# Who begins the copies of the kept weight sums, and a third seven-product unit in the attention's output projection

## The chip, the cores and the metric

The kernel runs on one core of one Trainium2 chip. The metric is device time in microseconds (us), the median of several executions. Engines are named as the profile names them: PE (TensorE, matmuls; PEld is its weight load), DVE (VectorE), ACT (ScalarE), POOL (GpSimd) and SP (SyncE, which here only begins DMA transfers). ACT and POOL can begin transfers too. Sixteen DMA engines carry the transfers of all three.

## The reference

Two layers of a pre-norm encoder trunk over 256 tokens of width 2048, all float32, and a last RMSNorm. Cut to what matters:

```python
h = x
for i in range(2):
    a = rms_norm(h, mix_norm[i])
    mixed = neighborhood_attention(a, na_w_qkv, na_rpb, na_w_o) if i == 0 \
            else short_conv_mixer(a, sc_w_in, sc_conv_w, sc_w_out)
    h = h + mixed
    h = h + conv_glu_ffn(rms_norm(h, ffn_norm[i]), ffn_w_up[i], ffn_conv_w[i],
                         ffn_conv_b[i], ffn_w_down[i])
return rms_norm(h, final_norm)
# attention: 16 heads of 128; output projection out (256x2048) @ w_o (2048x2048)
# ffn: up 2048 -> 2 x 5632, conv over 3 positions, silu(g)*u, down 5632 -> 2048
```

## The kernel before, in words

**Split products.** Every weight is read from HBM once per use and split on the chip into a high part `hi` (a rounding to float32r by ACT, line 186) and a low part `lo` (the rest, by DVE, line 189). Activations are split too. A product of two 128x128 by 128x512 blocks is then three matmuls: hi by hi, hi by lo, lo by hi (lines 463 to 465).

**Chunks.** Weights come in chunks, each loaded by SP into a tile `raw` (six buffers, 128x1024 at most) and then split into `hi` and `lo` tiles. The list `chunks` is in order of use. `prep_to(n)` writes out the loads and splits up to chunk n; the main loop calls it ahead of every item of PE's work, so that 4 chunks (AHEAD) or, in the up-projections and the short-convolution input, 6 chunks (FURTHER) are prepared ahead of the one in use. A load must wait until the splits have read the buffer that it fills. Each engine executes its own instructions in the order written; a planner sets this order, and `issue_after` ties an instruction behind a named one on the same engine.

**Phases.** Projections in which the weights stand still run as `Phase` (lines 262 and 270): q and k of the attention, the short convolution's input, and each FFN's up-projection in two halves. In a `Phase` an item is two output tiles of 128 channels, four chunks. v runs as `Values`, a pair of k blocks per item.

**Output projections** (attention's w_o, short convolution's w_out, and four half down-projections) run as `Tokens`: the activations stand still, 512 weight columns move. One group g covers 1024 output columns, in a left and a right half, and a unit is a pair of k blocks. An ordinary unit, P in the plans, takes eight block products in two chunks (left, right). A seven-product unit, H in the plans, is one step of Winograd's form of Strassen's method over two k blocks, two token blocks and two column halves: seven products instead of eight. It needs sums of weight blocks (the kept sums), sums of the activation blocks (`forms`, four adds on POOL, then a split), and four more PSUM accumulators `mu`, which `combine` adds into the result h once the last H unit of a group is done. `due` in the plan says how many ticks later that is written out. An H unit has three chunks: the left half, the second block of the right half, and the kept sums, whose loads fill two raw buffers (512 KB and 256 KB) and whose last sum is ended by one add on DVE (line 151).

**Kept sums.** The weight sums are made in DRAM by DMA, one job for each H unit and group (67 jobs). `make` writes a job out: three copies of 256 KB from the weight to the kept tile, later two transfers that add another block to them (`first`, 8 chunks later, ADDS) and one that adds a kept row to another (`second`, 16 chunks later). All six are begun by POOL, in POOL's own order (`pool`, line 217). The planning takes the jobs from one list, `jobs`, in order of use, and spreads them over earlier stages: QK_JOBS, V_JOBS, UP_JOBS and SC_JOBS say how many in each, and `hosts` over which items. Between these transfers POOL has the bias sums of the attention and the `forms`, each of which waits for a result of DVE or ACT; ahead of such a wait POOL issues whatever stands in its queue.

**Attention's tail.** `mix` (line 646 on) ends a pair of heads: PSUM tile o, split by ACT and DVE into `oT`, and for the pairs named in S_ATT a copy on ACT (line 667) and `make_forms`. The pairs of heads are the units of the output projection: unit 5 is heads 10 and 11. PSUM tiles `st`, `sc`, `tr`, `o` are used by the attention first and then by the `mu` sums. After a group of `Tokens` its results are added to h (line 360, `residual`), and this must be done before PE may start the next group on the same four PSUM tiles.

Of the kernel before, what the change touches and what calls it, by code (L numbers as in the profile page):

```python
# [26 lines left out]
NH = 16  # L27
# [18 lines left out]
def plan(text, due):  # L46


    words = text.split()
    return (tuple(int(x[1:]) for x in words), {int(x[1:]) for x in words if x[0] == "H"}, due)  # L50
# [4 lines left out]
S_MLP = {(0, 0): S_FIRST, (0, 1): (S_SECOND, S_SECOND),  # L55
         (1, 0): S_FIRST, (1, 1): (plan("P0 P2 H1 H3 H4 P9 H5 H6 H7 H8 P10", 0), plan("P0 P2 H1 H3 H4 P5 H6 H7 H8 P9 P10", 0))}
S_OUT = (plan("P0 H1 H2 P3 H4 H5 P6 P7", 1), plan("P0 P3 H1 H2 P6 H4 H5 P7", 0))
S_ATT = (plan("P0 P1 P2 H6 P3 H7 P4 P5", 1),) * 2
QK_JOBS, V_JOBS, UP_JOBS, SC_JOBS = (0, 2, 2, 0), (2, 2, 2, 0), (11, 11, 10, 11), 14


HEAD = (2, 4)
# [18 lines left out]
def trunk(ctx, tc, xT, par, bias, wqk, wv, wo, wsc, wscout, wup, wdown, out):  # L81
    nc = tc.nc
# [109 lines left out]
    kept, newest, fenced = {}, {}, []  # L192

    def make(w, g, i):

        kept[id(w), g, i] = dst = dp.tile([P, 3, 4 * P], F32, name=f"kept{len(kept)}")
        l, r, t = (w[8 * g + f:8 * g + f + 4, :, (2 * i + k) * P:(2 * i + k + 1) * P].rearrange("f p c -> p f c")
                   for f, k in ((0, 0), (4, 0), (4, 1)))
        at = [dst[:, n].rearrange("p (f c) -> p f c", f=4) for n in range(3)]
        for n, x in ((0, l), (1, t), (2, t)):  # L200
            pool(nc.gpsimd.dma_start, out=at[n], in_=x)

        def first():
            for n in range(2):
                pool(nc.gpsimd.dma_start, out=at[n], in_=r, accum_op=ALU.add)

        def second():
            pool(nc.gpsimd.dma_start, out=at[2], in_=at[0], accum_op=ALU.add)
        stores.append((len(prepped) + ADDS, first))
        stores.append((len(prepped) + 2 * ADDS, second))  # L210

    def pool(op, **of):

        with ExitStack() as order:
            if "POOL" in newest:
                order.enter_context(tc.issue_after(newest["POOL"].ins))
            newest["POOL"] = op(**of)  # L217
# [3 lines left out]
    def plan_jobs(w, plans):  # L221
        jobs.extend((w, g, i) for g, (order, sset, _) in enumerate(plans) for i in order if i in sset)

    def take(n):
        out, jobs[:] = jobs[:n], jobs[n:]
        return out
# [58 lines left out]
    at = [0]  # L285
# [19 lines left out]
    def split(dst, src):  # L305
        return split_into(dst[:, :S], dst[:, S:], src)
# [6 lines left out]
    def act_tile():  # L313
        return ap_.tile([P, 2 * S], F32R, name="act", tag="act", bufs=HALF)

    def a_tile():
        return ap_.tile([P, 2 * S], F32R, name="a", tag="a", bufs=KT)
# [202 lines left out]
    def make_forms(xe, xo, place, fresh=False):  # L520

        if fresh:
            form_at[:], left_over[:] = ("sf", "vv", "qk") * 2, ()
        v = tp.tile([P, 4, P], F32, name="s", tag="s")
        x11, x21, x12, x22 = (x[:, t * P:(t + 1) * P] for x in (xe, xo) for t in range(2))
        pool(nc.gpsimd.tensor_sub, out=v[:, 0, :], in0=x21, in1=x22)
        pool(nc.gpsimd.tensor_sub, out=v[:, 1, :], in0=v[:, 0, :], in1=x11)
        pool(nc.gpsimd.tensor_add, out=v[:, 3, :], in0=x12, in1=v[:, 1, :])
        pool(nc.gpsimd.tensor_sub, out=v[:, 2, :], in0=x11, in1=x21)
        if isinstance(place, tuple):  # L530
            hi, lo = place
            split_into(hi, lo, v.rearrange("p f c -> p (f c)"))
            return [(hi[:, j * P:(j + 1) * P], lo[:, j * P:(j + 1) * P]) for j in (0, 1, 3, 2)]

        blocks = 3 if place else 4
        y = form_slots(blocks)
        if isinstance(y, list):
            at = [(x[:, :P], x[:, P:]) for x in y]
            to = [(*at[j], v[:, j]) for j in range(3)]
        else:  # L540
            y = y.rearrange("p (b t c) -> p t b c", t=2, c=P)
            at = [(y[:, 0, j], y[:, 1, j]) for j in range(blocks)]
            to = [(y[:, 0, :blocks], y[:, 1, :blocks], v[:, :blocks])]
        if place:
            at.append((place[:, P:2 * P], place[:, 3 * P:]))
            to.append((*at[3], v[:, 3]))

        def splits():
            for x in to:
                split_into(*x)  # L550
        after(LATE, splits)
        return [at[j] for j in (0, 1, 3, 2)]
# [4 lines left out]
    def to_norm(n, a):  # L557

        ssq = ep.tile([P, 2, KT // 4], F32, name=f"ssq{n}")

        def evac(t, q, ps):
            added = residual(t, q, ps)
            squares(t, q, ssq)

            def next_input():
                for k0, tag in zip(range(4 * q - 4, 4 * q + 4, 2), ("tr", "o", "sc", "st")):
                    tr = transposed(k0, tag)
                    for k in range(2):
                        a[k0 + k] = a_tile()
                        scaled_split(a[k0 + k], tr[:, k, :], norm_g(n, k0 + k))  # L570
            if t and q % 2:
                after(1, next_input)
                if q == KT // 4 - 1:
                    after(2, lambda: spread_factor(token_factor(ssq)[0]))
            return added
        return evac
# [6 lines left out]
    oT = [None] * NH  # L583
# [67 lines left out]
    def mix(hs, v):  # L651

        o = pa.tile([P, 2, S], F32, name="o", tag="o")
        for i, h in enumerate(hs):
            for k in range(2):
                p = heads[h]["pT"][k]
                vh, vl = (x[:, h % 4 * P:(h % 4 + 1) * P] for x in v[k])
                nc.tensor.matmul(o[:, i, :], lhsT=vh, rhs=p[:, :S], start=k == 0, stop=False)
                nc.tensor.matmul(o[:, i, :], lhsT=vh, rhs=p[:, S:], start=False, stop=False)
                nc.tensor.matmul(o[:, i, :], lhsT=vl, rhs=p[:, :S], start=False, stop=k == 1)  # L660
        for i, h in enumerate(hs):
            oT[h] = act_tile()
            split(oT[h], o[:, i, :])
            heads[h].clear()
        if hs[0] // 2 in S_ATT[0][1]:
            x = tp.tile([P, 2, S], F32, name="s", tag="s")
            nc.scalar.copy(out=x, in_=o)

            place = (a_tile(), a_tile()) if hs[0] // 4 == NH // 4 - 1 else oT[hs[0]]
            oforms[hs[0] // 2] = make_forms(x[:, 0, :], x[:, 1, :], place)  # L670

    class Values:
# [175 lines left out]
    def mlp(layer, a, evac):  # L848
        for half in range(2):
            act, forms = [None] * HALF, {}  # L850
            lo = half * HALF
            Phase(wup[layer], [f for j in range(lo, lo + HALF) for f in (2 * j, 2 * j + 1)], KT, a,
                  up_evac(layer, act, forms, S_MLP[layer, half]), intro=0 if half else 3,
                  jobs=take(UP_JOBS[2 * layer + half]), hosts=(1, 20) if half else (4, 25))
            Tokens(down[layer, half], HALF, act, evac if half else residual, S_MLP[layer, half], forms,
                   halves=4 if half and layer else 0)

    down = {(layer, half): wdown[layer, half] for layer in range(2) for half in range(2)}
    plan_jobs(wo, S_ATT)
    for half in range(2):  # L860
# [4 lines left out]
    for g in range(NH // 4):  # L865
        Phase(wqk, range(8 * g, 8 * g + 8), KT, a0, qk_evac, intro=0 if g else INTRO, step=STEP,
              jobs=take(QK_JOBS[g]), hosts=(0, 4))
        Values(g, a0, take(V_JOBS[g]))
    Tokens(wo, KT, oT, to_norm(1, a1), S_ATT, oforms)
    mlp(0, a1, to_norm(2, a2))  # L870
# [52 lines left out]
    for item[0], (ph, ft, c, k0, ka, kb) in enumerate(items):  # L923

        with ExitStack() as order:
# [4 lines left out]
            if item[0] != KT // STEP * INTRO:  # L930
# [3 lines left out]
                end, n = ends[item[0]], FURTHER if getattr(ph, "fence", False) else AHEAD  # L934
# [77 lines left out]
```

## Time and profile before

| | us |
|---|---|
| median of 3 runs | 2210.82 (2210.37 to 2211.88) |
| the profiled execution, its time | 2210.34 |
| its span, first to last instruction | 2208.4 |
| PE busy | 2184.2 (99%) |
| DVE busy | 1744.9 (79%) |
| ACT busy | 1307.3 (59%) |
| POOL busy | 468.3 (21%) |

How to read it: the profile is one execution. Its page gives busy time by engine, forty slices of the span, the DMA queues, the chain of work that ended last, and the costliest groups of instructions. A busy PE is not PE at full rate: a 128x512 matmul is shown with some 391 ns, but matmuls overlap in the pipeline, so the rate is read from the starts of successive ones. The queue q1 holds what SP begins, q10 what ACT begins, q0 what POOL begins. A wait is put down to the releaser that came last.

The stages in the order of time: q, k and v up to 304 us, the attention's output projection up to 401, the first FFN (up, down, up, down) up to 1128, the short convolution up to 1481, the second FFN up to the end.

### The profile page before, as it was taken

The numbers are of one execution on the slowest core, as the hardware profiler recorded it, in microseconds if no ns is written. First come the engines' busy times: TensorE is split into PE (matmuls) and PEld (weight loads), VectorE is DVE, ScalarE is ACT, GpSimd is POOL, SyncE is SP. The second block draws the span as 40 slices with busy tenths as digits, with TensorE's granted clock in tenths as the row PEclk, the third lists the DMA queues.
The fourth block names the chain that finished last, engine by engine and source line by source line (L and its number), as shares of the span: only waits on it lengthen the run. The fifth ranks groups of instructions, "written<-read, shape, count | busy, mean of one in ns | idle before, by whom it ended". The sixth has DMA issues, their size and how long they took to land.

```text
span 2208.4 us, 33010 instructions
## 1 busy us (share of the span) xinstructions
PE 2184.2 (99%) x11707; PEld 1890.4 (86%) x11707; DVE 1744.9 (79%) x2664; ACT 1307.3 (59%) x1996; POOL 468.3 (21%) x561
## 2 busy tenths in 40 slices
PE   9999999999999999999999999999999999999998
PEld 8888887888888888887788888888888888888886
DVE  8777676877788887876986666888778898777898
ACT  7555555655566655654775544566556666555665
POOL 1343120024330023234001323101241100242200
PEclk9999999999999999999999999999999999999999
DMA  8999758688998879999876999966989887899885
GB/s 274 272 284 254 217 181 242 202 252 239 272 271 281 283 213 274 276 255 304 280 250 180 291 259 293 303 220 193 283 237 276 268 269 248 264 247 270 238 275 182
DMA packets 330389, 561.61 MB, mean 254 GB/s; under 512 B 22064, under 2 KB 219824, under 8 KB 330224
## 3 DMA queue, kind: packets, MB, share of 16 engines
q1 hardware_dynamic: 232368, 453.46, 60.3%
q0 software_dynamic: 96480, 105.41, 24.7%
q8 instruction: 92, 1.51, 0.3%
q10 hardware_dynamic: 1376, 0.63, 0.1%
q14 instruction: 73, 0.60, 0.1%
HBM read 557.32 MB, written 107.48 MB: 301 GB/s over the span
## 4 chain that ended last, share of the span: by engine, by line
PE 94%; DMA 2%; DVE 2%; ACT 1%; issue 1%; DVEq 0%; ACTq 0%
PE mm L262 42%; PE mm L270 22%; PE mm L463 6%; PE mm L464 6%; PE mm L465 6%; PE mu L463 2%; PE mu L465 2%; PE mu L464 2%; PE mm L693 1%; PE mm L694 1%; PE mm L695 1%; DVE lo L189 1%; DMA raw<-in_wo 1%; DMA raw<-in_wdown 1%; PE tr L371 1%
## 5 line engine op out<-in xcount | busy, mean ns | idle before, releaser
L189 DVE TENSOR_TENSOR lo<-raw,hi 128x1024 fp32r<-128x1024 f32 (+1 forms) x859 | 1021.0, 1214 | 194.0 <-PE mm L270 93.5
L186 ACT CAST hi<-raw 128x1024 fp32r<-128x1024 f32 (+1 forms) x926 | 923.4, 1010 | 421.1 <-PE mm L465 103.0
L262 PE MATMUL mm<-a,hi 128*128 128x512 f32 x4096 | 961.8, 391 | 0.5 <-DVE a L310 0.3
L262 PEld LDWEIGHTS mm<-a,hi 128*128 128x128 f32 x4096 | 759.7, 188 | 152.9 <-DVE a L310 1.2
L270 PEld LDWEIGHTS mm<-a,lo 128*128 128x128 f32 x4096 | 512.9, 192 | 11.8
L270 PE MATMUL mm<-a,lo 128*128 128x256 f32 x4096 | 518.1, 283 | 0.0
L217 POOL DMA_DIRECT2D kept<-in_wdown x275 | 276.5, 1672 | 88.8 <-DMA kept<-in_wdown 82.2
L463 PE MATMUL mm<-hi,act 128*128 128x512 f32 x620 | 243.4, 393 | 8.1 <-DVE h L360 7.4
L465 PE MATMUL mm<-hi,act 128*128 128x512 f32 x620 | 242.1, 391 | 0.0
L217 POOL TENSOR_TENSOR s<-conv 128x128 f32<-128x128 f32 x56 | 26.3, 470 | 952.1 <-DVE conv L752 952.1
L339 ACT ACTIVATE conv<-pad,pt 128x256 f32<-128x256 f32 x176 | 105.7, 601 | 194.7 <-DVE pad L331 194.5
L464 PE MATMUL mm<-lo,act 128*128 128x512 f32 x558 | 218.4, 391 | 0.9 <-DVE lo L189 0.8
L341 DVE SCALAR_TENSOR_TENSOR conv<-pad,pt,conv 128x256 f32<-128x256 f32 x384 | 185.2, 484 | 40.0 <-ACT conv L339 24.5
L325 ACT COPY corr<-mm 128x256 f32<-128x256 f32 x256 | 93.1, 369 | 135.8 <-PE mm L270 135.1
L463 PEld LDWEIGHTS mm<-hi,act 128*128 128x128 f32 x620 | 117.0, 189 | 34.1 <-issue 6.9
L465 PEld LDWEIGHTS mm<-hi,act 128*128 128x128 f32 x620 | 117.0, 189 | 24.3
L464 PEld LDWEIGHTS mm<-lo,act 128*128 128x128 f32 x558 | 105.4, 189 | 23.1 <-DVE lo L189 1.6
L302 DVE TENSOR_TENSOR act<-conv,act 128x256 fp32r<-128x256 f32 x88 | 37.7, 428 | 96.0 <-ACT act L301 96.0
L326 DVE TENSOR_TENSOR corr<-mm,corr 128x256 f32<-128x256 f32 x256 | 107.2, 420 | 5.6 <-ACT corr L325 5.5
L217 POOL DMA_DIRECT2D kept<-kept x67 | 70.6, 1072 | 126.6 <-DMA kept<-in_wdown 98.6
L463 PE MATMUL mu<-hi,sf 128*128 128x512 f32 x189 | 74.5, 394 | 1.9 <-ACT hi L186 1.9
L464 PE MATMUL mu<-lo,sf 128*128 128x512 f32 x189 | 74.6, 395 | 1.2 <-DVE lo L189 1.2
(156 smaller groups left out, 1658.0 us busy)
## 6 DMA issues: line engine op xcount, KB each, us to landing
raw<-in_wup SPq DMA_DIRECT2D x352, 512.0 KB, 6.3
kept<-in_wdown POOLq DMA_DIRECT2D x275, 256.0 KB, 12.9
raw<-in_wdown SPq DMA_DIRECT2D x121, 512.0 KB, 5.1
raw<-in_wsc SPq DMA_DIRECT2D x96, 512.0 KB, 6.4
raw<-kept SPq DMA_DIRECT2D x67, 512.0 KB, 5.5
raw<-in_wqk SPq DMA_DIRECT2D x56, 512.0 KB, 6.9
kept<-kept POOLq DMA_DIRECT2D x67, 256.0 KB, 8.5
raw<-kept SPq DMA_DIRECT2D x67, 256.0 KB, 4.9
```

The lines of the kernel that those rows point to most:

```text
L186: newest["ACT"] = nc.scalar.copy(out=hv, in_=r)
L189: newest["DVE"] = nc.vector.tensor_sub(out=lv, in0=r, in1=hv.bitcast(F32))
L217: newest["POOL"] = op(**of)
L262: nc.tensor.matmul(self.ps[ft], lhsT=prepped[i][0][:, o:o + P], rhs=self.src[k], start=k == 0, stop=False)
L270: nc.tensor.matmul(self.ps[ft][:, S:], lhsT=prepped[i][1][:, o:o + P], rhs=self.src[k][:, :S], start=False, stop=k == self.nk - 1)
L325: nc.scalar.copy(out=corr, in_=ps[:, S:])
L326: nc.vector.tensor_add(out=corr, in0=ps[:, :S], in1=corr)
L339: nc.scalar.activation(c, x[:, 1:S + 1], AF.Identity, scale=w[1], bias=b)
L341: nc.vector.scalar_tensor_tensor(out=c, in0=x[:, tap:tap + S], scalar=w[tap], in1=c, op0=ALU.mult, op1=ALU.add)
L463: nc.tensor.matmul(ps, lhsT=xh, rhs=wh, start=start, stop=False)
L464: nc.tensor.matmul(ps, lhsT=xh, rhs=wl, start=False, stop=False)
L465: nc.tensor.matmul(ps, lhsT=xl, rhs=wh, start=False, stop=stop)
```

## The change

Three things are edited. The three copies of each job are begun by ACT, tied behind the newest hi split that was written out, instead of by POOL in POOL's order; the adding transfers stay on POOL. The attention's output projection gets a third H unit, unit 5, in both groups, another order of units, and `due` 0 instead of 1; that makes 69 jobs instead of 67, and the two more are taken in the second half of the first FFN's up-projection. The forms of unit 5 get two `act` tiles of their own.

```diff
-S_ATT = (plan("P0 P1 P2 H6 P3 H7 P4 P5", 1),) * 2
-QK_JOBS, V_JOBS, UP_JOBS, SC_JOBS = (0, 2, 2, 0), (2, 2, 2, 0), (11, 11, 10, 11), 14
+S_ATT = (plan("P0 P1 H5 P2 H6 P3 H7 P4", 0),) * 2
+QK_JOBS, V_JOBS, UP_JOBS, SC_JOBS = (0, 2, 2, 0), (2, 2, 2, 0), (11, 13, 10, 11), 14
...
         for n, x in ((0, l), (1, t), (2, t)):
-            pool(nc.gpsimd.dma_start, out=at[n], in_=x)
+            with tc.issue_after(newest["ACT"].ins):
+                nc.scalar.dma_start(out=at[n], in_=x)
...
-            place = (a_tile(), a_tile()) if hs[0] // 4 == NH // 4 - 1 else oT[hs[0]]
+            place = tuple((a_tile if hs[0] // 4 == NH // 4 - 1 else act_tile)() for _ in range(2))
```

## The prediction

> **What bounds the kernel now.** I read the busy times first, then the rows of who waited for whom on PE, then stretches of the trace beside each other.
>
> ```profile
> PE 2184.2 (99%) x11707; PEld 1890.4 (86%) x11707; DVE 1744.9 (79%) x2664; ACT 1307.3 (59%) x1996; POOL 468.3 (21%) x561
> ...
> PE mm L463 <- DVE h L360: 7.4, 3, 5.4
> PE mu L464 <- DVE lo L189: 2.0, 3, 0.8
> PE mu L463 <- ACT hi L186: 1.9, 1, 1.9
> ```
>
> PE is the bound, and it hardly waits: one wait of 5.4 us, and a handful of small ones. So a gain must come from fewer matmuls, or from the few places where PE is starved. The stretches show these places. The rows are the attention's output projection, then three half down-projections with the same count of products: first FFN, halves one and two, and second FFN, half one. Columns: stretch, length, busy us and instructions of PE, PEld, DVE, ACT, POOL, granted clock, DMA share, GB/s.
>
> ```profile
> 304.60:401.00 96.40, 91.03 (x414) 75.49 (x413) 67.59 (x81) 51.94 (x72) 17.12 (x21) 0.96 0.75 221
> 647.90:758.10 110.20, 110.20 (x489) 91.26 (x488) 94.57 (x106) 68.74 (x76) 4.14 (x5) 1.00 0.89 287
> 1002.50:1128.50 126.00, 118.28 (x504) 93.89 (x503) 103.19 (x123) 76.01 (x95) 19.70 (x20) 0.97 0.97 289
> 1728.00:1838.20 110.20, 110.20 (x488) 91.27 (x488) 94.54 (x107) 68.84 (x77) 0.00 (x0) 1.00 0.84 275
> ```
>
> The third takes 126.0 us where its twins take 110.2, and in it and in the first the clock is below 1.00 and POOL is busy. What POOL does there, in its order of time (start, length, count):
>
> ```profile
> 317.76 2.87 POOL L217 TENSOR_TENSOR s<-s 128x128 f32<-128x128 f32 x4 [3.27 <-ACT s L667]
> 320.57 4.50 POOL L217 DMA_DIRECT2D kept<-in_wdown  x6
> 325.31 7.39 POOL L217 DMA_DIRECT2D kept<-in_wdown  x7 [0.25 <-issue]
> ...
> 994.39 4.79 POOL L217 DMA_DIRECT2D kept<-in_wscout  x6
> 1002.59 8.22 POOL L217 DMA_DIRECT2D kept<-in_wscout  x8 [3.42 <-DMA kept<-in_wscout]
> ```
>
> With its last adds of the stage before done, POOL has nothing to wait for and begins the kept-sum transfers of the next stage at once: 13 from 320.6 on, 20 in the stretch from 1002.5 on. The weights' loads pay for it. Median time from issue to landing, whole run first, then 320 to 356, then whole run, then 1002 to 1050; after them ACT's waits in 320 to 356 and in 1018 to 1072:
>
> ```profile
> raw<-in_wo SPq DMA_DIRECT2D x28, 512.0 KB, 4.9
> raw<-in_wo SPq DMA_DIRECT2D x11, 512.0 KB, 12.4
> raw<-in_wdown SPq DMA_DIRECT2D x121, 512.0 KB, 5.1
> raw<-in_wdown SPq DMA_DIRECT2D x7, 512.0 KB, 11.6
> ...
> ACT hi L186 <- DMA raw<-in_wo: 13.7, 7, 3.7
> ACT hi L186 <- DMA raw<-in_wdown: 16.3, 11, 3.5
> ```
>
> Late loads make late splits, DVE comes late to the group's end (line 360), and PE stands. At the first place, on PE:
>
> ```profile
> 349.55 0.39 PE L465 MATMUL mm<-hi,act 128*128 128x512 f32 x1
> 355.31 0.77 PE L463 MATMUL mm<-hi,act 128*128 128x512 f32 x1 [5.37 <-DVE h L360]
> 355.87 0.63 PE L464 MATMUL mm<-lo,act 128*128 128x512 f32 x1
> ...
> 358.85 0.39 PE L465 MATMUL mm<-hi,act 128*128 128x512 f32 x1
> 359.08 0.39 PE L463 MATMUL mm<-hi,act 128*128 128x512 f32 x1
> 359.77 1.91 PE L371 MATMUL tr<-pt,h 128*128 128x128 f32 x16
> ```
>
> Successive starts are 0.23 us apart when all is well (358.85 to 359.08), not the 0.39 that one matmul is shown with.
>
> **The change part by part.**
>
> *The copies leave POOL's run ahead.* ACT is in order and busy with splits, so a copy goes out when the chunk before it in the list is split. The jobs that ran at 320 belong to the up-projection that starts at 401, those at 1002 to the convolution from 1128 on; tied to ACT they go out there. The adding transfers stay on POOL, but wait for the copies, so they move too. What that gives back:
> - First place: the gap 349.55 to 355.31 less one normal step, 5.76 - 0.23 = 5.53 us. Then the eight matmuls from 355.31 to 358.85 take 3.54 us where 8 x 0.227 = 1.82 would do: 1.72 us at a lower clock. Together 7.25.
> - Second place: 126.0 - 110.2 = 15.8 us against the twin, less the 16 transposes that only this stage has, 1.9 by the row above: 13.9 us.
> Late next at both places is nothing that I can find: the twins run with DVE at 94.5 of 110.2 us and PE without a gap, and loads at 275 to 287 GB/s.
>
> The Trainium skill (DMA: Bandwidth & Descriptors, "Issuing engines are not separate DMA queues") says that transfers begun by different engines share the same 16 DMA engines, and that spreading them only saves time at the issuing sequencer. By that rule alone, with the same bytes at the same moments, this term would be zero. The load rows above agree that the engines are shared; what the change moves is the moment.
>
> *What it costs on ACT.* 69 x 3 = 207 issues. No long series of issues on ACT is in this trace, so I bound one by SP's issues of the same kind (min, median, max in ns) and by POOL's of these very copies:
>
> ```profile
> L165 SPq DMA_DIRECT2D raw<-in_wdown x176: 367/383/2747, 624.3 to 2178.1; - x176
> L165 SPq DMA_DIRECT2D raw<-in_wo x32: 367/378/4395, 278.6 to 380.4; - x32
> L217 POOL DMA_DIRECT2D kept<-in_wo x20: 748/786/2346, 60.2 to 129.9; - x20
> ...
> 850.00:900.00 50.00, 50.00 (x288) 44.18 (x287) 38.50 (x68) 30.18 (x50) 19.42 (x26) 1.00 0.97 268
> 425.77 7.28 PE mm L262 x32
> 433.05 3.83 PE mm L270 x32
> ...
> kept<-in_wdown POOLq DMA_DIRECT2D x275, 256.0 KB, 12.9
> ACT sf L301 <- POOL s L217: 34.5, 32, 1.2
> ```
>
> Usual price 0.38 us, so 1.1 us a job and 207 x 0.38 = 79 us of ACT in all. An up-projection item takes 7.28 + 3.83 = 11.11 us and `hosts` spreads 10 to 14 jobs over 19 to 23 items, one in 16 to 23 us; ACT is busy 30.18 of 50 us there, so it has some 8 us free in 20. Behind the issue wait the next splits, the copies out of PSUM and the convolution's first tap; DVE waits for these, and PE for DVE. PE has four to six chunks in hand, 11 to 16 us (an item is four chunks). 1.1 us is hidden: 0. The upper end is an issue that is held up for 2.7 to 4.4 us, as SP's slowest: three of them are 8.2 to 13.2 us. The medians of 0.38 say that this is rare, so I take 0, and allow 0.5 us for the three `Values` stages, where two jobs stand only two chunks apart. The lower end is a small gain: DVE and ACT lose no time to slow loads. POOL saves 201 x 0.79 = 158 us, worth nothing: it is 21% busy.
>
> *The queues it is moved past.* On POOL the adds of a job now wait for copies that ACT begins, and the bias adds and `forms` stand behind them; ACT waits for `forms` (last row but one gives 12.9 us to land; the last row is that wait, 1.2 us at most now). The adds are written out 8 chunks after the copies, 8 x 11.11/4 = 22 us: 12.9 fits, so 0; a landing of over 22 us would pass on to ACT. On SP nothing is moved, but its loads share the engines with ACT's copies as they did with POOL's: same bytes, 0.
>
> *The third unit.* Two more H units, each with three matmuls of 512 columns less: 2 x 3 x 0.2275 (7.28/32) = 1.37 us off PE. For it each H unit adds DVE work: half a chunk less than two more chunks, and one add.
>
> ```profile
> L189 DVE TENSOR_TENSOR lo<-raw,hi 128x1024 fp32r<-128x1024 f32 x843 | 1010.4, 1224 | 191.9 <-PE mm L270 93.5 <-ACT hi L186 87.4 <-issue 5.6
> L186 ACT CAST hi<-raw 128x1024 fp32r<-128x1024 f32 x843 | 874.0, 1048 | 379.0 <-PE mm L262 94.0 <-PE mm L465 70.5 <-DMA raw<-in_wup 52.4
> L189 DVE TENSOR_TENSOR hi<-raw,hi 128x512 fp32r<-128x512 f32 x67 | 46.4, 692 | 18.6 <-ACT hi L186 18.2
> L151 DVE TENSOR_TENSOR raw<-raw 128x512 f32<-128x512 f32 x67 | 46.5, 693 | 1.9
> ```
>
> An ordinary unit costs DVE 2 x 1.22 = 2.4 us, an H unit 3 x 1.22 + 0.69 + 0.69 = 5.0; so 2.6 more in each group, and 1.6 on ACT. The stage had DVE at 67.6 of 96.4 us; 73 of some 88 leaves room, less tight than the twins (94.5 of 110.2). The two more jobs bring 12 transfers of 256 KB into a stage with a DMA share of 0.97 that PE did not feel: 0. Forms of unit 5 (an ACT copy, four POOL adds of 2.9 us together by the row above, a split) lie in the fourth q,k stage, where PE is never starved: 0. `due` 0 writes `combine` one item earlier, before the last unit, as in the twin from 647.9 on the whole: 0, with a bound of a lost group change, some 3 us.
>
> *Sum.* -7.25 - 13.9 - 1.37 + 0.5 = -22.0 us on the profiled execution's 2210.34 (span 2208.4 and 1.9 around it), 2188.3. The median of the runs is 0.5 higher, so 2188.8, say 2189.
>
> **The rivals.**
>
> *Half of it.* The collisions at one place stay: late adds or the last jobs of an up-projection fall into the projection behind it, where H units want their loads fastest. For it: each up-projection hosts jobs nearly to its end and `second` comes 16 chunks later. Against it: at 644.67 eight such transfers ran into the stage from 647.9 on, and it lost nothing.
>
> ```profile
> 644.67 4.81 POOL L217 DMA_DIRECT2D kept<-in_wdown  x6
> 651.54 2.56 POOL L217 DMA_DIRECT2D kept<-in_wdown  x2 [2.05 <-DMA kept<-in_wdown]
> ```
>
> Times: 2189 + 7.25 = 2196 with the first place unchanged, 2189 + 13.9 = 2203 with the second.
>
> *The collision only moves.* The copies meet the up-projections' loads, or SP's loads stand behind copies that land late, and PE loses there what it gains. For it: the DMA share is already 0.97 in the row from 850 on. Against it: that same row has PE at 50.00 of 50.00. Time: 2206 to 2215, no change. The rule of the Trainium skill weighed above would give this case, if the engines were full at all times; the stretches above show shares from 0.75 to 0.97.
>
> *ACT is held by its issues (slower).* Place: ACT's queue in the stages with jobs. For it: SP's slowest issues, 2.7 and 4.4 us. Against it: medians of 0.38 us. Per job ACT has 8 us free in 20; three issues reach that at 2.7 us each, the slowest of SP's in_wdown rows. At 3.2 us each they would want 9.6, 1.6 us over for each of the 59 jobs behind the attention: 94 us, 2189 + 94 = 2283. It decides from 2.7 us on; the result passes the old time at 3 x 2.8 = 8.4, 0.4 over, 59 x 0.4 = 24 us.
>
> **How the numbers follow.** Sum as forecast, 0.66 (2186 to 2193). Half of it, 0.15. Collision only moves, 0.09: within 0.2% (4.4 us, about what a measurement of this kernel tells from no change) 0.07, slightly slower 0.02. ACT held, 0.08. Something else slower, a split order that the planner makes worse, 0.02. Faster by over 0.2% is the first two, 0.81; same 0.07; slower 0.12. The range has to leave out no more than 2 in 10: it runs from 2185 to 2204. The upper end is that of the half cases. The lower is the sum without the 0.5, and 3 us more out of the 11 us in which PE is idle outside the two places (2208.4 - 2184.2, less 5.4 and 7.7), should loads that land sooner shorten those too.
>
> **What would show it.** Stretches: the attention's projection about 88 us long, the second down-projection about 112, both with clock 1.00 and few POOL transfers in them. Loads of in_wo land in some 5 us throughout. PE's wait for line 360 of 5.4 us gone. Issues on ACT near 0.38 us each, no wait of PE on line 186. Matmuls 11707 - 6 = 11701. Wrong would be: ACT issues of microseconds, ACT waiting for POOL's `forms` for more than a few us, clock below 1.00 in new places.

## The result, and the profile after

| | before | changed |
|---|---|---|
| median, us | 2210.6 (2209.3 to 2211.88) | 2187.33 (2186.53 to 2187.66) |
| profiled execution, span, us | 2208.4 | 2185.2 |

The ratio is 0.9894, with an interval of 0.9877 to 0.9911: 23.3 us less, where 21.8 less were forecast. One more run of before is in its row than above. Each experiment's ratio, too, is against runs of the kernel before on the experiment's own chip, whose medians were 2209.5 to 2212.0, and "less" is counted from them.

First the busy times on the changed kernel's page, then what PE waited for (total us, times, longest). The changed file is one line longer from line 201 on (in `make`), so the old lines 262, 360 and 463 are 263, 361 and 464 here, and 186 is still 186.

```profile
PE 2174.1 (99%) x11701; PEld 1886.6 (86%) x11701; DVE 1749.0 (80%) x2671; ACT 1313.2 (60%) x2002; POOL 326.9 (15%) x370
```

```profile
PE bc L811 <- DVE conv L809: 1.6, 1, 1.6
PE tr L794 <- DVE h L361: 1.1, 1, 1.1
PE st L114 <- DVE inv L770: 1.1, 1, 1.1
PE mm L263 <- ACT hi L186: 0.4, 1, 0.4
```

PE has six matmuls less, and its wait of 5.4 us for the group's end is gone; what is left is small, and the three rows of over 1 us stand at the start and the end of the run. The stretches are those of the prediction: attention's projection, first FFN's down-projection halves one and two, and the row from 850 on; then the two stages that took the moved transfers in, the first half of that FFN's up-projection and the short convolution's input. Columns: stretch, length, busy us and instructions of PE, PEld, DVE, ACT, POOL, granted clock, DMA share, GB/s.

```profile
304.30:392.00 87.70, 87.70 (x407) 73.16 (x406) 69.30 (x85) 53.99 (x73) 5.57 (x8) 1.00 0.69 217
638.90:749.10 110.20, 110.20 (x488) 91.25 (x487) 94.56 (x107) 68.65 (x76) 0.00 (x0) 1.00 0.81 267
993.60:1105.50 111.90, 111.90 (x504) 92.92 (x503) 102.33 (x122) 76.02 (x95) 0.00 (x0) 1.00 0.82 268
850.00:900.00 50.00, 50.00 (x282) 43.95 (x281) 39.84 (x71) 30.21 (x49) 13.81 (x17) 1.00 1.08 278
...
392.00:639.00 247.00, 247.00 (x1428) 218.57 (x1427) 200.63 (x341) 153.03 (x251) 51.68 (x61) 1.00 0.93 257
1105.00:1375.00 270.00, 270.00 (x1560) 238.90 (x1559) 187.85 (x299) 137.72 (x202) 54.91 (x58) 1.00 0.99 272
```

The projection went from 96.4 to 87.7 us and the second down-projection from 126.0 to 111.9; the twin between them stayed at 110.2. Clock and PE are whole in all six, and POOL begins nothing in the down-projections. Where the packets went is in the next rows: the stretch 318 to 356 first, with SP's loads alone in it and 4.6 us to land (12.4 before), then the second down-projection from 994 to 1042, then the whole run's rows of the copies (ACT) and of the adds (POOL). Last column: median us from issue to landing.

```profile
q1 hardware_dynamic: 7890, 8.32, 67.9%
...
raw<-in_wo SPq DMA_DIRECT2D x12, 512.0 KB, 4.6
```

```profile
raw<-in_wdown SPq DMA_DIRECT2D x14, 512.0 KB, 4.9
...
kept<-in_wdown ACTq DMA_DIRECT2D x165, 256.0 KB, 7.0
...
kept<-in_wdown POOLq DMA_DIRECT2D x110, 256.0 KB, 12.0
```

POOL in order of time, at the place where 13 transfers went out at 320 before. Now its next transfer starts at 394, after a wait of 73 us for ACT's copies:

```profile
317.72 2.87 POOL L218 TENSOR_TENSOR s<-s 128x128 f32<-128x128 f32 x4 [3.27 <-ACT s L668]
...
394.07 2.55 POOL L218 DMA_DIRECT2D kept<-in_wdown  x2 [73.49 <-DMA kept<-in_wdown]
```

**Where the 23.2 us of span came from.** Counting on PE how much later each matmul starts than the usual spacing would have it, PE lost 29.65 us before and 8.0 after, and its matmuls at that spacing take 1.4 us less. The first place gave 7.2 (7.3 lost before, 0.1 after), the second 13.9 (nothing left), the third unit 1.4. That is 22.5; some 0.7 us are small pieces elsewhere.

### The profile page after: what moved, and what is told of

Read it like the earlier page. It is cut to its first block, busy times and chain, and to the rows that moved or that the text cites. A ratio compares the mean times of both kernels' runs of the same rounds, so it can differ in the third digit from the quotient of the medians.

```text
span 2185.2 us, 33213 instructions
## 1 busy us (share of the span) xinstructions
PE 2174.1 (99%) x11701; PEld 1886.6 (86%) x11701; DVE 1749.0 (80%) x2671; ACT 1313.2 (60%) x2002; POOL 326.9 (15%) x370
## 4 chain that ended last, share of the span: by engine, by line
PE 98%; DVE 1%; ACT 0%; DMA 0%; issue 0%; SPq 0%; DVEq 0%; ACTq 0%
PE mm L263 43%; PE mm L271 22%; PE mm L464 6%; PE mm L466 6%; PE mm L465 6%; PE mu L464 3%; PE mu L466 3%; PE mu L465 3%; PE mm L694 1%; PE mm L696 1%; PE mm L695 1%; PE tr L372 1%; PE tr L647 0%; DVE lo L189 0%; DMA raw<-in_wqk 0%; DVE a L817 0%
## 5 line engine op out<-in xcount | busy, mean ns | idle before, releaser
L464 PE MATMUL mm<-hi,act 128*128 128x512 f32 x610 | 238.1, 390 | 0.0
L466 PE MATMUL mm<-hi,act 128*128 128x512 f32 x610 | 237.4, 389 | 0.0
L218 POOL DMA_DIRECT2D kept<-in_wdown x110 | 150.5, 1820 | 487.9 <-DMA kept<-in_wdown 487.8
L465 PE MATMUL mm<-lo,act 128*128 128x512 f32 x546 | 212.6, 389 | 0.0
L464 PEld LDWEIGHTS mm<-hi,act 128*128 128x128 f32 x610 | 114.6, 188 | 23.7 <-DVE h L361 0.4
L466 PEld LDWEIGHTS mm<-hi,act 128*128 128x128 f32 x610 | 114.5, 188 | 23.7
L332 DVE TENSOR_TENSOR pad<-corr,rstd 128x256 f32<-128x256 f32 x176 | 74.3, 423 | 0.1
```

The lines of the kernel that those rows point to most:

```text
L464: nc.tensor.matmul(ps, lhsT=xh, rhs=wh, start=start, stop=False)
L465: nc.tensor.matmul(ps, lhsT=xh, rhs=wl, start=False, stop=False)
L466: nc.tensor.matmul(ps, lhsT=xl, rhs=wh, start=False, stop=stop)
```

## The experiments

The theory was: what costs is the moment at which the copies go out, POOL's run ahead into a projection that needs its loads fast. A job's adds wait for its copies, so every experiment that moves copies moves their adds too; none moves one kind alone. The rivals were that ACT's queue or its transfers are better in themselves, that the third unit does part of it, and that ACT is near its limit.

**1. The copies alone** (kernel before, with one edit).

```diff
-            pool(nc.gpsimd.dma_start, out=at[n], in_=x)
+            with tc.issue_after(newest["ACT"].ins):
+                nc.scalar.dma_start(out=at[n], in_=x)
```

> The copies begun by ACT, the attention's plan as before (two H units, due 1, 67 jobs). Theory (the moment of the copies): both starved places go, 7.25 + 13.9 = 21.2 us, so 2210.6 - 21.2 = 2189.4. Rival (the first place went because the attention's units were put in another order): only the second goes, 2210.6 - 13.9 = 2196.7.

Measured: 2188.63 us, ratio 0.9896 (0.9882 to 0.9911), 22.7 less. Its stretches, projection and second down-projection:

```profile
304.50:393.60 89.10, 89.10 (x413) 74.36 (x412) 67.50 (x81) 51.77 (x72) 5.29 (x8) 1.00 0.64 202
...
995.00:1107.00 112.00, 112.00 (x505) 93.03 (x504) 102.41 (x122) 76.45 (x95) 0.00 (x0) 1.00 0.83 269
```

Both places close with this edit alone. The projection is 1.4 us longer than with the third unit: that is what the unit is worth on top.

**2. The third unit alone** (kernel before, with the new plan, the new numbers of jobs and the new tiles; copies still on POOL).

> The new plan of the attention's projection and its 69 jobs, the copies still begun by POOL in its run ahead. Theory: 1.4 us of matmuls less, both starved places stay: 2209.2, PE's gap ahead of line 361 between 300 and 400 us still some 5 us. Rival (order): the first place goes with the new order, 1.4 + 7.25 less, 2202.

Measured: 2214.3 us, ratio 1.0011 (1.0002 to 1.0020): some 3 us slower than before, not 1.4 faster. A miss. PE's waits and ACT at 1005:

```profile
304.50:401.20 96.70, 91.51 (x407) 74.97 (x406) 69.72 (x85) 54.22 (x73) 17.40 (x21) 0.96 0.78 231
...
1002.90:1132.70 129.80, 119.08 (x505) 95.12 (x504) 105.43 (x126) 78.31 (x99) 17.48 (x19) 0.96 0.96 284
```

```profile
PE mm L463 <- DVE h L360: 6.9, 4, 4.3
PE mm L463 <- DVE corr L326: 6.1, 1, 6.1
```

```profile
1004.89 1.05 ACT L186 CAST hi<-raw 128x1024 fp32r<-128x1024 f32 x1 [3.43 <-DMA raw<-in_wdown]
```

The six matmuls less are there (407 where the first experiment has 413), yet the stretch is 96.7 us long, as before: by the count of the section above PE loses 9.2 us in it, where it lost 7.3 before, and gives the gain back. That three H units per group want more of the late loads in the same time is a likely reason, not a shown one. The second place grows by 3.8 us; two more jobs end the up-projection there, and a new gap of 6.1 us stands at 1005, where ACT waits for a load. So this edit has its worth only when the copies keep out of the way; the run does not part the unit from its two jobs.

**3. POOL begins the copies, in step with the splits** (changed kernel). POOL first reads one column of the newest split, and so waits as ACT would:

```diff
+        newest["hi"] = hi[:, :1]
...
+        pool(nc.gpsimd.tensor_copy, out=ep.tile([P, 1], F32, name="step", ...),
+             in_=newest["hi"].bitcast(F32))
...
-            with tc.issue_after(newest["ACT"].ins):
-                nc.scalar.dma_start(out=at[n], in_=x)
+            pool(nc.gpsimd.dma_start, out=at[n], in_=x)
```

> The changed kernel with the copies back on POOL, but each job's copies stand behind a one-column copy on POOL that reads the newest hi split, so POOL begins them when ACT would. Theory (the moment): as the changed kernel, 2187.3, up to 2 us more where POOL's forms stand behind. Rival (who begins them: software-begun copies of 4 KB packets are what holds the loads): most of the 21 us stay, 2203 or more.

Measured: 2190.62 us, ratio 0.9907 (0.9890 to 0.9923), 3.3 us above the changed kernel where 2 were allowed. What POOL waits for at the added line, and the longest of PE's waits that the changed kernel has not:

```profile
POOL step L219 <- ACT hi L186: 638.6, 20, 129.9
...
PE mm L465 <- DVE corr L328: 1.1, 1, 1.1
```

POOL is held back for 638.6 us in all, and 20 of the 23 us come with it, although the engine and the queue are those of before. The moment makes the gain; that it is ACT who begins them is worth 3 us at most.

**4 and 5. One place at a time** (kernel before). ACT begins only the copies of the short convolution's `wscout` (4), or all but these (5):

```diff
+            if w is wscout:        # 5: if w is not wscout:
+                with tc.issue_after(newest["ACT"].ins):
+                    nc.scalar.dma_start(out=at[n], in_=x)
+            else:
+                pool(nc.gpsimd.dma_start, out=at[n], in_=x)
```

> The kernel before, with only the eight jobs of the short convolution's output (24 of 201 copies) begun by ACT. Theory (the burst beside the second down-projection is all of the loss there): 13.9 us less, 2196.7, the gap at 350 us stays. Rival (lighter traffic everywhere is what helps): 24/201 of 21.2 us, 2.5 less, 2208.

> The kernel before, with all copies begun by ACT but those of the eight jobs of the short convolution's output, which stay in POOL's order. Theory (two bursts, each with its own loss): the first place goes (7.25 us), and the second stays (13.9 us), since those copies still run ahead: 2203. Rival (with POOL's order held up by adds that wait for ACT's copies, the remaining copies on POOL are no longer run ahead, and both places go): 2189.

Measured: (4) 2195.19 us, ratio 0.9927 (0.9912 to 0.9942), 16.1 less; (5) 2200.94 us, ratio 0.9957 (0.9942 to 0.9971), 9.2 less. First both stretches of (4), then both of (5):

```profile
303.80:399.00 95.20, 90.84 (x414) 75.35 (x414) 67.59 (x81) 51.91 (x72) 17.12 (x21) 0.98 0.76 224
...
1000.60:1112.60 112.00, 112.00 (x505) 92.92 (x504) 104.06 (x124) 75.86 (x94) 0.00 (x0) 1.00 0.82 268
```

```profile
304.00:393.10 89.10, 89.10 (x414) 74.30 (x413) 67.52 (x81) 51.78 (x73) 5.31 (x8) 1.00 0.63 202
...
994.50:1119.50 125.00, 117.99 (x504) 93.97 (x503) 105.23 (x125) 75.93 (x97) 15.15 (x16) 0.97 0.97 285
```

Each place goes with its own copies and stays without them, as the prediction's two terms have it. Together they give 25.3, 2.6 more than the first experiment's 22.7. Most of that is visible: the place that is left loses less than it did (95.2 us for 96.4 in (4), where the lower clock lasted 3.4 us instead of 6.8; 125.0 for 126.0 in (5)).

**6. SP begins the copies** (changed kernel).

```diff
-            with tc.issue_after(newest["ACT"].ins):
-                nc.scalar.dma_start(out=at[n], in_=x)
+            load(at[n], x)
```

> The changed kernel with the copies begun by SP, in the order of its loads, instead of by ACT. Theory (what counts is that they are not run ahead): 2187.3, within 1.5 us. Rival (it must be ACT, since on SP every copy stands ahead of a load): loads land late, ACT waits for them longer than the 93 us or so now, 2191 or more.

Measured: 2198.35 us (2194.32 to 2200.99), ratio 0.9944 (0.9927 to 0.9961), some 11 us worse than the changed kernel. ACT's waits, first with SP, then the same two rows of the changed kernel:

```profile
ACT hi L186 <- DMA raw<-in_wup: 83.0, 55, 5.1
...
ACT hi L186 <- DMA raw<-in_wsc: 36.5, 24, 5.7
```

```profile
ACT hi L186 <- DMA raw<-in_wup: 31.3, 30, 2.3
...
ACT hi L186 <- DMA raw<-in_wsc: 16.9, 17, 1.7
```

```profile
PE mm L463 <- DVE corr L326: 3.5, 2, 2.1
PE mm L262 <- DVE a L310: 2.9, 4, 1.8
```

The rival's number came out. SP's order does not run ahead of the chunks either, so "anything but POOL's run ahead" is not enough. On SP the three copies stand ahead of the loads of the next chunks; the splits wait 71 us longer for weights, and a part of that reaches PE (the last two rows, SP's kernel). The profiled execution, 2195.77, shows some 9 of the 11 us; the rest lies in executions without a profile.

**7. Twice the issues on ACT** (changed kernel; each copy in two halves of 64 rows, the same bytes).

> The changed kernel with each copy in two halves of 64 rows, so ACT begins 414 transfers instead of 207, with the same bytes. Theory (an issue of 0.56 us on ACT lies beside PE): some 116 us more on ACT at most, time 2187.3, within 1 us. Rival (ACT is near the point from which it holds PE): 2191 or more, with PE waiting for ACT's splits.

Measured: 2201.4 us, ratio 0.9959 (0.9944 to 0.9974): 14 us worse, as the rival had it. ACT in order of time at the start of the up-projection, the same at the start of the short convolution, and PE's longest wait:

```profile
397.02 9.55 ACTq L203 DMA_DIRECT2D kept<-in_wdown  x6
406.61 1.04 ACT L186 CAST hi<-raw 128x1024 fp32r<-128x1024 f32 x1 [8.56 <-DMA kept<-in_wdown]
...
1118.20 7.29 ACTq L203 DMA_DIRECT2D kept<-in_wscout  x6
1125.53 1.04 ACT L186 CAST hi<-raw 128x1024 fp32r<-128x1024 f32 x1 [6.30 <-DMA kept<-in_wscout]
```

```profile
PE mm L264 <- ACT hi L186: 7.9, 2, 5.0
```

An issue is shown with a median of 0.62 us here too, six would take 3.7; they take 9.55, and ACT's idle time before the split is ended by an earlier copy's landing. In the records ACT's and SP's transfers count up one set of eight semaphores in turn, and an issue waits until the older transfer on its semaphore has landed: the last three issues begin at 402.27, 404.11 and 406.01, and the older transfers landed at 402.25, 404.09 and 405.99. The second of these is a load of SP's. PE waits 5.0 us at the first place and 2.9 at the second, and its clock falls to half at both; by the count above they cost 7.5 and 4.6 us more than in the changed kernel, most of the 14.

**8. ACT busy instead** (changed kernel). To tell issue time from waiting, six copies of 128x96 per job on ACT, 414 in all, that nobody needs:

```diff
+        for _ in range(6):
+            with tc.issue_after(newest["ACT"].ins):
+                nc.scalar.copy(out=ep.tile([P, 96], F32, name="idle", ...), in_=ones[:, :96])
```

> The changed kernel with six small copies (128x96) on ACT behind each job's three issues, read by nobody: some 1.6 us of ACT time a job, 110 us in all, as much as the doubled issues cost, and no transfer more. Theory (ACT's time is hidden, and the doubled issues lost their 14 us in waiting on ACT for an earlier transfer to land): 2187.3, within 1.5 us. Rival (ACT's time itself is what PE felt): 2198 or more.

Measured: 2186.74 us, ratio 0.9893 (0.9878 to 0.9908), no loss. The added copies (min, median, max in ns) and the stretch behind the projection:

```profile
L205 ACT COPY idle<-ones x414: 255/273/282, 51.3 to 2015.6; 128x96 f32<-128x96 f32 x138
...
395.00:415.00 20.00, 20.00 (x118) 17.65 (x117) 15.02 (x28) 14.12 (x32) 4.52 (x4) 1.00 1.12 276
```

414 x 0.273 = 113 us more on ACT cost nothing, so the loss of experiment 7 is not ACT's time; what is left of it is the standing still for transfers that its rows show.

**9. The collision brought back, with copies begun by ACT** (changed kernel). Four jobs of the first up-projection are written out between the units of the attention's projection:

```diff
-QK_JOBS, V_JOBS, UP_JOBS, SC_JOBS = (0, 2, 2, 0), (2, 2, 2, 0), (11, 13, 10, 11), 14
+QK_JOBS, V_JOBS, UP_JOBS, SC_JOBS = (0, 2, 2, 0), (2, 2, 2, 0), (7, 13, 10, 11), 14
...
-    Tokens(wo, KT, oT, to_norm(1, a1), S_ATT, oforms)
+    Tokens(wo, KT, oT, to_norm(1, a1), S_ATT, oforms, jobs=take(4))
```

> The changed kernel with four jobs of the first up-projection begun by ACT between the units of the attention's projection, so twelve copies and their adds fall where POOL's thirteen fell before. Theory (the moment is what costs): a good part of the 7.25 us at that place comes back, 2191 to 2196, clock 0.5 for a while near 350 us. Rival (hardware-begun copies of 512 bytes a run give way to the loads): nothing comes back, 2187.3 to 2188.5.

Measured: 2199.97 us, ratio 0.9956 (0.9940 to 0.9973), 12.6 us worse, more than expected. The stretch, PE at the group's change, POOL's adds, and loads and queue shares from 318 to 356:

```profile
303.80:404.50 100.70, 90.71 (x407) 73.86 (x406) 70.22 (x86) 55.14 (x74) 18.66 (x20) 0.95 0.92 249
```

```profile
359.34 0.77 PE L466 MATMUL mm<-hi,act 128*128 128x512 f32 x1 [8.84 <-DVE h L361]
...
321.31 10.18 POOL L218 DMA_DIRECT2D kept<-in_wdown  x8
```

```profile
q0 software_dynamic: 4796, 3.14, 59.9%
q10 hardware_dynamic: 1675, 0.83, 7.5%
...
raw<-in_wo SPq DMA_DIRECT2D x9, 512.0 KB, 13.9
```

The whole picture of before is back: in_wo landing in 13.9 us, PE waiting for the group's end, the clock at 0.95. But ACT's copies are not what met the loads there: all twelve had landed by 322.6 us, 28 us before PE's gap. What ran beside the loads are POOL's adds (q0), eight begun together at 321.3 and four more behind them. By the packets, the eight took 17.0 us of all sixteen engines' time and the four 5.6; before, in 320 to 356, q0 had nine copies with 7.4 us and four adds with 8.2. So this run shows that the moment of a job's adds costs, and why the loss is larger than expected; it does not test copies begun by ACT beside these loads, and no run here tells how much of the first place was copies and how much adds.

**10, 11 and 12. A fourth H unit in both groups** (changed kernel). Each takes six more matmuls away. (10) has unit 4 too, and two more jobs in the first FFN; (11) spreads the jobs otherwise; (12) has another order of units.

```diff
-S_ATT = (plan("P0 P1 H5 P2 H6 P3 H7 P4", 0),) * 2
+S_ATT = (plan("P0 P1 H4 H5 P2 H6 H7 P3", 0),) * 2      # 12: P0 P1 H4 H5 H6 H7 P2 P3
# jobs of 10: UP_JOBS (12, 14, 10, 11); of 11 and 12: QK_JOBS (0, 2, 2, 2), UP_JOBS (12, 12, 10, 11)
```

> The changed kernel with a fourth H unit (unit 4) in both groups of the attention's projection, order P0 P1 H4 H5 P2 H6 H7 P3, 71 jobs (12 and 14 in the two halves of the first up-projection). Theory (matmuls alone, everything else still hidden): 2 x 3 x 0.2275 = 1.4 us less, 2185.9. Rival (two H units in a row, and 26 activation tiles wanted of 22, starve PE): 2189 or more.

> The kernel with the fourth H unit and two of its jobs moved from the second up-projection half (14 to 12) to the fourth q,k stage. Theory (the fourth unit gave nothing because the last of 14 jobs ran into the end of that half, 1.8 us of PE at 995 us): the gap at 995 goes, 2185.5. Rival (it is the fourth unit's own load on its projection): 2187.5 as before.

> The kernel with the fourth H unit and its jobs spread, order P0 P1 H4 H5 H6 H7 P2 P3 instead of P0 P1 H4 H5 P2 H6 H7 P3, so that two ordinary units stand behind the last H unit of a group. Theory (the fourth unit's matmuls are saved, and DVE, busy without a break from 334 to 352 us, is late to the group's end for 1.5 us and more): with a longer cover for the combine the gap at 349 goes, 2185.1. Rival (four H units in a row starve PE before): 2187 or more, waits of PE for splits between 318 and 340 us.

Measured: (10) 2187.48 us, ratio 0.9899 (0.9885 to 0.9914); (11) 2187.10, 0.9894 (0.9878 to 0.9911); (12) 2188.44, 0.9893 (0.9876 to 0.9909). None can be told from the changed kernel. PE's new wait in each, in that order:

```profile
PE mm L464 <- DVE corr L327: 1.4, 1, 1.4
```

```profile
PE mm L464 <- DVE h L361: 1.1, 1, 1.1
```

```profile
PE mu L464 <- DVE a L311: 1.1, 1, 1.1
```

Each time some 1.4 us of matmuls went and a gap of 1.5 to 1.8 us between two starts came: at 995, where two more jobs end the second up-projection (10); at the group's change at 349, with DVE busy without a break from 334 on (11); in the next group at 361 (12). Mending one gap opened another. No version here beats the changed kernel by more than a measurement can tell.

## Why the prediction was right

It said 2189.0 (2185 to 2204); measured were 2187.33.

- **First place, -7.25, and third unit, -1.37.** The projection is 8.7 us shorter, for 8.62 forecast; experiment 1 gives the first 7.3, the difference to the changed kernel 1.4.
- **Second place, -13.9.** 126.0 to 111.9, against a forecast of about 112. Taking a twin stage as the measure of what an undisturbed one takes was right to 0.2 us. Experiments 4 and 5 tie each place to its own copies.
- **The moment, not the engine.** Held: POOL in step keeps 20 of 23 us (3), and four jobs at the wrong moment cost 12.6 us, by adds that POOL begins as in the changed kernel (9). The prediction speaks of the copies; how much of the two terms was theirs and how much the adds' stays open. By the Trainium skill (DMA: Bandwidth & Descriptors, "Issuing engines are not separate DMA queues") the issuer gives no bandwidth of its own. Experiment 3 agrees, to 3 us. Experiment 6 shows what that leaves open: with the same bytes near the same moments, the copies in SP's order, ahead of its loads, cost 11 us.
- **Terms taken as independent.** Here the working was weak. The -1.37 stands only with the copies in step; on the kernel before, the same edit costs 3 us (2). The sum came out because both edits were made, and to that extent by luck.
- **The allowance of 0.5 us** was not needed; this and the 0.7 us of small pieces are most of the miss of 1.5.
- **ACT's issues.** Mis-sized. Taken was 0.38 us, SP's price for a load. Issues of the kept tile on ACT (most of the 207; min, median, max in ns), and the same copies begun by SP in experiment 6:

```profile
L202 ACTq DMA_DIRECT2D kept<-in_wdown x165: 558/560/2517, 151.2 to 2011.7; - x165
...
L165 SPq DMA_DIRECT2D kept<-in_wdown x165: 552/636/6233, 139.1 to 2010.5; - x165
```

 A copy is dearer than a load on SP too, so the load was the wrong measure, not SP. 207 x 0.56 = 116 us for the forecast 79, and nothing of it is felt; 113 us more would not be either (8).
- **The rival "ACT is held by its issues"** had its point of decision in the wrong quantity: 2.7 us per issue. What holds ACT is an issue that waits for an older transfer, and the changed kernel has such holds already, at 1301 nearly as long as in experiment 7:

```profile
1300.78 8.03 ACTq L202 DMA_DIRECT2D kept<-in_wdown  x3
1308.93 2.00 ACT L186 CAST hi<-raw 128x1024 fp32r<-128x1024 f32 x2 [7.11 <-DMA kept<-in_wdown]
```

 That one lies in the middle of a stage, with chunks in hand, and PE does not feel it; in experiment 7 holds of 8.6 and 6.3 us fell on the starts of two stages and cost PE waits of 5.0 and 2.9 us at once. In these runs what decides is where the hold falls.
- **POOL behind ACT's copies: 0.** Held. The 12.9 us to land that the prediction took for the copies is the median of a row of 165 copies and 110 adds; the copies alone, picked out by POOL's order, took 13.8, which still fits its 22. POOL waits up to 139 us for them, and ACT's longest wait for POOL's forms is still 1.2 us. **SP: 0.** Right in the sum, but not for the reason given: SP now does wait for copies, up to 10.0 us, and no wait of PE follows from it. POOL's, ACT's and SP's rows (total, times, longest):

```profile
POOL kept L218 <- DMA kept<-in_wdown: 600.6, 31, 139.0
...
ACT sf L302 <- POOL s L218: 14.9, 16, 1.2
```

```profile
SPq L165 <- DMA kept<-in_wdown: 59.6, 13, 10.0
```

- **The rivals "half of it" and "the collision only moves".** In the changed kernel's trace neither copies nor adds move a byte in the attention's projection until 391.3 us, its last microsecond, or in the second down-projection. The two stages that took them in have PE at 247.00 of 247.00 and 270.00 of 270.00, at DMA shares of 0.93 and 0.99.

## What to carry to other kernels

A queue that has nothing to wait for begins its work at the earliest moment, not the right one: where a background transfer meets a stage that needs its loads fast, tie it (and what is begun behind it) to the progress of the main work, on whichever engine can do that without standing ahead of the loads. Compare a slow stage with its twin to price the repair, and look at loads' landing times by stretch, since the whole run's median hid a factor of 2.5. Put such transfers on a compute engine's queue only in the middle of stages, where its standing still for a landing is covered by work in hand, and price a gain in matmuls only after the loads that it needs are known to be on time.

## What the runs showed of the hardware

- An issue of a 256 KB copy from DRAM to DRAM took a median of 0.56 us on ACT and 0.64 on SP (experiment 6), where SP's loads of `wdown` took 0.38; six in a row on ACT took 9.55 us when older transfers had not landed.
- The copies of `wdown` landed in 7.0 us when ACT began them, in 13.8 when POOL did (before); the moments differ too. In the records ACT's went as runs of 512 bytes, 27 ns each at the median, POOL's as packets of 4096 bytes, 165 ns each. The adds went as packets of 512 bytes, 65 ns each: in 320 to 356 before, four of them took 8.2 us of all sixteen engines' time and nine copies 7.4.
- At the group's change of the projection the granted clock fell to 0.50 some 2.1 us after PE fell idle (before, and experiment 9) or 3.9 us after (experiment 4). It stayed there for 6.8, 10.2 and 3.4 us, the last 3.0 to 3.5 of them with PE at work again: matmuls 0.43 us apart instead of 0.23. So the gap before cost 1.7 us more than its length, while the single gaps of 1.1 to 1.4 us of experiments 10 to 12 left no such trace on the clock. At the second place it fell too, with no long gap ahead of it: before at 1041.5 us, for 6.8 us, after gaps of 1.9 us at most; in experiment 2 at 1044.4, for 3.4 us, after gaps of 0.9 us at most. The Trainium skill (TensorE: Matmul & The Clock Gate, "Part 1: The HAM clock gate (the "warmup" mystery)") has activity judged in free-running windows of some 3.4 us: the three lengths, all multiples of 3.4, agree. It has the low clock come after a whole idle window; here 2.1 us of idleness were enough, and at the second place less in one piece.
